# Twenty-eight projection groups ahead of the first attention score, bounded due times in the planner, and gated slots in program order, in a two-layer decoder trunk

## The chip, the cores and the metric

The kernel runs on one core of one Trainium2 chip. The metric is the device time of one execution in microseconds; less is better. Times are given as the median of several runs. One further execution was recorded by the hardware profiler; all rows quoted below come from such a record. The engines are TensorE (PE; its weight loads are PEld), VectorE (DVE), ScalarE (ACT), GpSimd (POOL) and SyncE (SP), whose queue issues the DMAs.

## The reference, cut to what matters

The input is x of 1024 tokens by 1024 features, 256 memory tokens, and weights, all fp32. Two layers follow each other. Layer 0 mixes by native sparse attention with 12 heads of 64 in two groups: queries and six key and value sets are projected, queries and keys are rotated, and each query attends to compressed blocks, to selected blocks and to a window. Layer 1 mixes by forgetting attention over shared keys and values. Both layers attend with four further heads to the memory tokens, project the heads' output, and end with a gated feed-forward part whose up-projection is followed by a causal convolution of width 3.

```python
proj = h @ w_in                                  # 1024 x 1024 by 1024 x A_IN
q = rope(proj[..., :MIX_W].reshape(B, S, 12, 64), pos)
...
s = jnp.einsum('btghd,bngd->bghtn', qc, kc).astype(jnp.float32) * scale
p_cmp = masked_softmax(s, cmp_end[None, :] <= t[:, None])
...
return g[..., 0:1] * o_cmp + g[..., 1:2] * o_slc + g[..., 2:3] * o_win
```

## The kernel before, in words

**Arithmetic.** Every fp32 operand of a matmul is kept as a high and a low part. ScalarE writes the high part (`upper`, L86), VectorE the low part (`lower`, L92). `mm3` (L166, L167, L168) adds three matmuls, high by high, high by low, low by high. One such triple over one of eight tiles of the contraction is called a group here; it is 128 x 512 of output.

**Stages.** Per layer: a projection, the attention, a seam that holds the output projection and prepares the feed-forward part, the gated up-projection (`Up.run`), and the down-projection (`Down`). Layer 0's projection is `layer0_proj` and its attention `attention0`.

**Layer 0's attention.** The projection ahead of it makes keys, values and the first block of queries, rotates them (VectorE L1056, L1057, L1062, POOL L1063), stores them to DRAM (SP L1067) and loads them in another layout (kk by L1258, vv by L1265, qq by L1273). A unit of attention is then a row of tiles: scores (TensorE L316), a lift that masks and takes the maximum (VectorE L356), exponentials (ScalarE L376), weighing by the inverse sums (POOL L411), transposes of the probabilities (TensorE L448) whose result is split into parts (ScalarE L459, VectorE L462), and products with the values (TensorE L475).

The next query blocks (q1, q2) and the memory queries (m0, m1) are projected inside the attention: 96 groups as filler between scores and products. `advance()` puts the next group into the list. Before the first unit, four are put at each early step; afterwards the rest is spread evenly over the steps. Each block of such filler brings its weight loads (L710), conversions, a rotation (VectorE L739, POOL), and stores (SP).

**The planner.** `attention0` and `seam` do not issue instructions at once. They add nodes to an `Order`: engine, assumed cost, due time, the nodes to come after, and the buffers held. `play` then simulates the five engines with these costs and picks for each engine, among the nodes that are ready first, the one due first. The nodes are issued in the order that results, and TensorE, VectorE, ScalarE and GpSimd keep it. SP's queue is placed by the framework from the order of issue.

**The gated up-projection.** It makes the tiles of `Up.run` in slots, seven products per column pair (`product(n, 0)` to `product(n, 6)`), each of four groups. The first four products of columns 0 and 1 are made in the seam. The two halves p and c of a column's accumulator live in psa, of which there are two. `place_early` copies the first sum to its place on GpSimd (L2007), `copied` takes an accumulator half out on ScalarE (L1980). Weight sums come from GpSimd (L1939, L1940, L1946, L1947) and are converted by ScalarE and VectorE. TensorE's order in these slots is chosen by the framework's scheduler, which may interleave products.

Of the kernel before, what the change touches and what calls it, by code (L numbers as in the profile page):

```python
# [44 lines left out]
class Trunk:  # L45
# [590 lines left out]
    def attention0(self, ap, cpool, h, w, od, units, work, spare, lead, lag=2):  # L636
# [142 lines left out]
        def begin(it):  # L779
# [63 lines left out]
            if "norm" in it:  # L843
                i0, i1 = it["norm"]
                brs = u["branches"][i0:i1]
                inv = o.add("DVE", 0.18, lambda: self.invert(u, i0, i1), lambda: min(firsts[id(b), i].due for b in brs for i in b["spans"]) - 3,
# [101 lines left out]
        parts = list(ahead())  # L948
        first = min(it["at"] for it in items)
# [342 lines left out]
    def seam(self, l, oT, pool, fx, up):  # L1292
# [120 lines left out]
        def turn(t):  # L1413
# [17 lines left out]
            c = o.add("POOL", 1.35, lambda: gt(half(u, 0), half(t, 1), half(u, 0), ALU.subtract), due("t3", 6.5 - u), [b])  # L1431
            d = o.add("POOL", 1.35, lambda: gt(half(u, 1), half(u, 1), half(t, 1), ALU.subtract), due("t4", 6.5 - u), [b, s["raw", u, 1]])
# [16 lines left out]
        def sums_21(n, due, behind=()):  # L1449
# [10 lines left out]
            a = o.add("POOL", 1.35, one, due, [lb, *behind], [h, hb], early=20.0)  # L1460
            s["21", n] = o.add("POOL", 1.35, two, due, [a, la], [h, ha], early=20.0)

        def sums_34(n, due):
# [10 lines left out]
            a = o.add("POOL", 1.35, one, due, [la, lb], [h, ha, hb], early=20.0)  # L1474
            s["34", n] = o.add("POOL", 1.35, two, due, [a, s["21", n]], [h, ha, g], early=20.0)
# [421 lines left out]
class Up:  # L1897
# [110 lines left out]

    def third(self, n):
        s = self.st[n]  # L2010
        self.prod(n, s["p"], "s2", "t2", False)
        s["c2"] = self.copied(s["p"])
# [64 lines left out]
    def run(self, late, down):  # L2077
# [28 lines left out]
        for slot in range(7 * NF + 13):  # L2106
            for f in todo.pop(slot, ()):
                f()
            for n in (slot // 7 - 1, slot // 7):
                i, odd = divmod(slot - 7 * n, 2)  # L2110
                if 0 <= n < NF and not odd and done.get(n, 0) <= i < 7:
                    self.product(n, i)
            if slot >= 7 * NF + 6:
                down.step()
# [109 lines left out]
class Hold:  # L2224

    def __init__(self, tag):
        self.tag, self.users, self.left, self.taken = tag, [], 0, False
# [9 lines left out]
class Order:  # L2237

    SHARED = 0.6
    HOP = {"SP": 2.3, "PE": 0.23, "ACT": 0.15, "DVE": 0.14, "POOL": 0.08}  # L2240

    def __init__(self, room):
        self.room, self.nodes, self.queue = room, [], {}

    def hold(self, tag, keep=False):
        h = Hold(tag)
        if tag != "psb":
            self.queue.setdefault(tag, []).append(h)
        h.left = 10 ** 9 if keep else 0
        return h  # L2250

    def held(self, tag):
        h = Hold(tag)
        h.taken = True
# [3 lines left out]
    def add(self, eng, cost, fn, due, after=(), holds=(), early=10.0, slow=False):  # L2258
        n = Node(eng, cost, fn, due, [a for a in after if a is not None], early, slow)
        for h in holds:  # L2260
            h.users.append(n)
            h.left += 1
# [3 lines left out]

    def seen(self, n, eng):

        return n.end + (0.0 if n.eng == eng != "SP" else self.HOP[n.eng])

    def play(self):

        left, free = {}, {}
        for n in self.nodes:
            if callable(n.due):
                n.due = n.due()
            left.setdefault(n.eng, []).append(n)
# [3 lines left out]
        slots = {t: [0.0] * k for t, k in self.room.items()}  # L2281
        drift, out = 0.0, []
        while any(left.values()):
            best = None
            for eng, ns in left.items():
                ready = []
                for n in ns[:160]:
# [5 lines left out]
                    if any(h.tag in self.queue and h not in self.queue[h.tag][:want.count(h.tag)] for h in takes):  # L2293
# [3 lines left out]
                    for x in set(want):  # L2297
                        t = max(t, sorted(slots[x])[want.count(x) - 1])
# [8 lines left out]
            n.start, n.end = t, t + n.cost  # L2307
# [4 lines left out]
            for h in n.holds:  # L2312
                if not h.taken:
                    h.taken = True
                    slots[h.tag].remove(min(slots[h.tag]))
                    if h.tag in self.queue:
                        self.queue[h.tag].remove(h)
                h.left -= 1
                if h.left == 0:
                    slots[h.tag].append(max(self.seen(u, None) for u in h.users))  # L2320
# [61 lines left out]
```

## Time and profile before

| what | us |
|---|---|
| median of 3 runs | 2527.55 |
| lowest and highest of them | 2522.82, 2528.29 |
| profiled execution, its own time | 2525.68 |
| its span in the trace | 2523.7 |
| TensorE busy | 2430.8 |
| VectorE busy | 1875.6 |
| ScalarE busy | 1352.6 |
| GpSimd busy | 730.7 |

A row of a timeline gives start, length, engine, line, operation, output<-inputs and tile, and in brackets how long the engine stood idle before and what ended that. A row of windows gives a stretch of the span, its length, the busy time and count of PE, PEld, DVE, ACT and POOL, then TensorE's granted clock as a share of full speed, the share of time in which the DMA engines were busy, and GB/s. A row on waits gives the engine and line that waited, what it waited for, the total, the number of times and the longest. Matmuls overlap, so the step from start to start is shorter than the length of one.

### The profile page before, as it was taken

How to read it: one execution, taken by the hardware profiler on the slowest of the kernel's cores; microseconds unless marked ns; L12 is line 12 of the kernel's file. 1: busy time of each engine (PE TensorE's matmuls, PEld its weight loads, DVE VectorE, ACT ScalarE, POOL GpSimd, SP SyncE). 2: the span in 40 equal slices, each digit the busy share in tenths (PEclk: the TensorE clock that was granted, in tenths of full speed). 3: DMA queues.
4: the chain of work that ended last, by engine and by line, in shares of the span. 5: the costliest groups of instructions: out<-in, count | busy, mean ns of one | idle time of the engine just before them, and what ended most of it. 6: DMA issues, size and time to landing. Idle time of an engine off the chain costs nothing. (4 is left out here: it accounts for less than half of the span.)

```text
span 2523.7 us, 35482 instructions
## 1 busy us (share of the span) xinstructions
PE 2430.8 (96%) x12210; PEld 2042.2 (81%) x12210; DVE 1875.6 (74%) x3182; ACT 1352.6 (54%) x2583; POOL 730.7 (29%) x620
## 2 busy tenths in 40 slices
PE   7969999998989999999999999998999999999998
PEld 6768888887778888888889988887777888888886
DVE  5747888887487787879765467878577777788765
ACT  5325888886354544544454356756255444445444
POOL 0103455555145554540000000000225455451000
PEclk9989999999999999999999999999999999999999
DMA  8464233245613333358335566765613333238533
GB/s 250 141 193 144 60 84 87 78 133 158 209 59 104 105 112 97 100 177 303 92 126 157 151 187 194 200 177 182 230 76 96 100 100 113 92 109 306 170 95 123
DMA packets 303276, 357.68 MB, mean 142 GB/s; under 512 B 38024, under 2 KB 183288, under 8 KB 303096
## 3 DMA queue, kind: packets, MB, share of 16 engines
q1 hardware_dynamic: 303096, 355.41, 44.8%
q8 instruction: 97, 1.59, 0.3%
q14 instruction: 83, 0.68, 0.1%
HBM read 245.55 MB, written 109.78 MB: 141 GB/s over the span
## 5 line engine op out<-in xcount | busy, mean ns | idle before, releaser
L2046 DVE SCALAR_TENSOR_TENSOR v<-u,cw,v 128x1023 f32<-128x1023 f32 (+1 forms) x176 | 270.6, 1537 | 67.8 <-ACT v L2044 66.1
L86 ACT ACTIVATE wh<-wr 128x512 fp32r<-128x512 f32 (+2 forms) x244 | 182.2, 751 | 240.8 <-PE psa L168 109.7
L92 DVE TENSOR_TENSOR wl<-wr,wh 128x512 fp32r<-128x512 f32 (+2 forms) x244 | 228.5, 940 | 110.3 <-ACT wh L86 110.0
L462 DVE TENSOR_TENSOR pt<-psb,pt 128x512 fp32r<-128x512 f32 (+2 forms) x380 | 246.3, 659 | 61.8 <-ACT pt L459 59.8
L2044 ACT ACTIVATE v<-u,cw 128x1024 f32<-128x1024 f32 x88 | 109.6, 1245 | 308.1 <-DVE u L2033 282.6
L459 ACT ACTIVATE pt<-psb 128x512 fp32r<-128x512 f32 (+2 forms) x380 | 214.2, 576 | 107.4 <-PE psb L448 104.0
L166 PE MATMUL psa<-hT,wh 128*128 128x512 f32 x560 | 218.9, 391 | 12.5 <-ACT wh L86 9.5
L475 PE MATMUL psb<-pt,vv 128*128 128x512 f32 (+2 forms) x864 | 218.5, 354 | 8.3 <-DVE pt L462 6.1
L168 PE MATMUL psa<-hT,wl 128*128 128x512 f32 x560 | 218.0, 389 | 0.8 <-DVE wl L92 0.8
L167 PE MATMUL psa<-hT,wh 128*128 128x512 f32 x560 | 218.2, 390 | 0.0
L316 PE MATMUL psa<-kk,qq 128*128 128x512 f32 (+4 forms) x792 | 176.4, 342 | 24.9 <-DMA qq<-qd 20.2
L356 DVE CUSTOM_DVE_ANT_0 ps<-psa,caub 128x128 f32<-128x128 f32 (+1 forms) x192 | 139.7, 751 | 36.6 <-PE psa L316 26.4
L376 ACT ACTIVATE ps<-ps,stat 128x128 f32<-128x128 f32 (+1 forms) x192 | 148.0, 776 | 27.9 <-DVE stat L356 27.5
L475 PEld LDWEIGHTS psb<-pt,vv 128*128 128x128 f32 x864 | 136.9, 189 | 26.9 <-DVE pt L462 11.8
L316 PEld LDWEIGHTS psa<-kk,qq 128*128 128x128 f32 x792 | 123.4, 192 | 43.2 <-issue 20.2
L166 PE MATMUL psb<-hT,wh 128*128 128x512 f32 x384 | 157.5, 410 | 0.4 <-DVE pt L462 0.4
L130 POOL TENSOR_TENSOR rs<-ss,consts 128x1 f32<-128x1 f32 x24 | 13.3, 555 | 491.5 <-DVE ss L128 319.5
L168 PE MATMUL psb<-hT,wl 128*128 128x512 f32 x384 | 151.8, 395 | 0.0
L167 PE MATMUL psb<-hT,wh 128*128 128x512 f32 x384 | 151.4, 394 | 0.0
L448 PE MATMUL psb<-consts,ps 128*128 128x128 f32 x928 | 146.3, 274 | 3.7 <-POOL ps L411 1.3
L539 POOL TENSOR_TENSOR wr<-wr 128x512 f32<-128x512 f32 x16 | 22.1, 1386 | 408.3 <-ACT wh L216 240.7
L166 PE MATMUL psa<-hx,wh 128*128 128x512 f32 x352 | 138.6, 394 | 0.0
(320 smaller groups left out, 6773.7 us busy)
## 6 DMA issues: line engine op xcount, KB each, us to landing
wr<-in_w_up_dram SPq DMA_DIRECT2D x88, 512.0 KB
wr<-gd SPq DMA_DIRECT2D x154, 256.0 KB
gd<-v SPq DMA_DIRECT2D x88, 256.0 KB
o<-ob SPq DMA_DIRECT2D x128, 128.0 KB
wr<-o SPq DMA_DIRECT2D x32, 512.0 KB
hT<-in_w_down_dram SPq DMA_DIRECT2D x64, 256.0 KB
gd<-gs SPq DMA_DIRECT2D x60, 256.0 KB
qd<-st SPq DMA_DIRECT2D x56, 256.0 KB
```

The lines of the kernel that those rows point to most:

```text
L86: self.nc.scalar.activation(hi, src, AF.Copy)
L92: self.nc.vector.tensor_tensor(lo, src, f32(hi), ALU.subtract)
L166: mm(out, lh, rh, start=first, stop=False, skip_group_check=more)
L167: mm(out, lh, rl, start=False, stop=False, skip_group_check=more)
L168: mm(out, ll, rh, start=False, stop=last, skip_group_check=more)
L316: nc.tensor.matmul(out, w, rhs, start=b not in banks[:i], stop=b not in banks[i + 1:])
L376: nc.scalar.activation(p, p, AF.Exp, bias=st[:, 0, ii:ii + 1], scale=-1.0, accum_out=st[:, 1, ii:ii + 1])
L448: nc.tensor.transpose(tp[0:kb, x:x + P], br["pt"][ii][:, o:o + kb], self.ident)
L459: nc.scalar.activation(st["hi"], st["src"], AF.Copy)
L462: self.nc.vector.tensor_tensor(st["lo"], st["src"], f32(st["hi"]), ALU.subtract)
L475: self.nc.tensor.matmul(out, v, t, start=st["begin"] and i == 0, stop=st["end"] and i == len(mms) - 1)
L2046: nc.vector.scalar_tensor_tensor(v[:, d:], u[:, :S - d], cw[:, tap, i:i + 1], v[:, d:], ALU.mult, ALU.add)
```

## The change

There are three parts.

**The front of layer 0's attention.** Ahead of the first unit a node without instructions is added for SP (assumed cost 12, due at -1), and 28 groups of filler are put into TensorE's list by `advance()`. The weights of a query block are fetched two units of planner time earlier.

```
-                d = o.add("SP", 0.45, fetch, now, holds=[wr], early=14.0)
+                d = o.add("SP", 0.45, fetch, now - 2, holds=[wr], early=14.0)
...
         parts = list(ahead())
+        o.add("SP", 12.0, lambda: None, -1.0)
+        for _ in range(28):
+            advance()
         first = min(it["at"] for it in items)
```

On TensorE, at the end of the projection ahead of the attention, the rows before are these (psb_1593 is the last projection, hT the normalized input, kk and qq keys and queries):

```order
L167 MATMUL psb_1593<-hT_92,wh_1124 128x512
L168 MATMUL psb_1593<-hT_91,wl_1125 128x512
L316 MATMUL psa_1703<-kk_261_1660,qq_265_1674 128x128
L316 MATMUL psa_1703<-kk_261_1660,qq_266_1675 128x128
L316 MATMUL psa_1703<-kk_261_1660,qq_265_1674 128x256
L316 MATMUL psa_1703<-kk_261_1660,qq_266_1675 128x256
L316 MATMUL psa_1703<-kk_261_1660,qq_265_1674 128x384
L316 MATMUL psa_1703<-kk_261_1660,qq_266_1675 128x384
L316 MATMUL psa_1713<-kk_261_1660,qq_265_1674 128x512
L316 MATMUL psa_1713<-kk_261_1660,qq_266_1675 128x512
L166 MATMUL psb_1727<-hT_89,wh_1710 128x512
```

At the same place they are now these (psb_1675, psb_1701, psb_1742 and psb_1795 are the filler's accumulators; of 84 filler matmuls the first three and the last three are shown):

```order
L168 MATMUL psb_1593<-hT_91,wl_1125 128x512
L166 MATMUL psb_1675<-hT_89,wh_1664 128x512
L167 MATMUL psb_1675<-hT_90,wh_1664 128x512
L168 MATMUL psb_1675<-hT_89,wl_1665 128x512
...
L166 MATMUL psb_1795<-hT_91,wh_1669 128x512
L167 MATMUL psb_1795<-hT_92,wh_1669 128x512
L168 MATMUL psb_1795<-hT_91,wl_1670 128x512
L316 MATMUL psa_1823<-kk_278_1768,qq_271_1721 128x128
L316 MATMUL psa_1823<-kk_278_1768,qq_272_1722 128x128
```

The first score stood directly behind the projection; now 84 filler matmuls stand between them. From the first score to the first L448 there are 48 groups before and after; behind that, 48 were left before and 20 are left now.

On SP, at the same place, the rows before (qd<-st stores the rotated queries; the others load):

```order
L1258 DMA kk_261_1660<-kd_80 32x1024 x2
L1067 DMA qd_79<-st_1639 128x512 x2
L1067 DMA qd_79<-st_1647 128x512 x2
L1258 DMA kk_261_1660<-kd_80 32x1024 x2
L1258 DMA kk_262_1665<-kd_80 32x8x128 x4
L1265 DMA vv_1670<-vd_81 128x8x128
L1265 DMA vv_1672<-vd_81 128x8x128
L1273 DMA qq_265_1674<-qd_79 32x512
L1273 DMA qq_266_1675<-qd_79 32x512
```

And now, where kk_278 is kk0, kk_277 is kk1, and seven loads of qq stand between the cos table and kk_277, of which the first two are shown:

```order
L661 DMA wr_1926<-in_a_w_in_dram 128x8x128
L1276 DMA qq_271_1721<-qd_79 32x512
L732 DMA sin_1716<-in_rope_dram 128x512
L1070 DMA qd_79<-st_1639 128x512 x2
L1070 DMA qd_79<-st_1647 128x512 x2
L732 DMA cos_1714<-in_rope_dram 128x512
L1276 DMA qq_272_1722<-qd_79 32x512
L1276 DMA qq_271_1721<-qd_79 32x512
...
L1261 DMA kk_277_1753<-kd_80 32x8x128 x4
L1261 DMA kk_278_1768<-kd_80 32x1024 x4
```

Behind the stores stood six loads of kk, two of vv and eight of qq; now a cos table, seven loads of qq and eight of kk stand there, and the loads of vv come later.

On VectorE the low parts of the first two weight blocks (wl, L92, four instructions) stood behind the first lift L356 and now stand among the last conversions of the projection. The first lift now stands behind the rotation (L739) of the first three filler accumulators, two instructions of each.

**The planner.** The assumed cost of the inversion goes from 0.18 to 0.30, those of GpSimd's sums in the seam from 1.35 to 1.6, and the share by which a busy GpSimd lengthens a VectorE node from 0.6 to 1.0. Due times are bounded by successors before the simulation, and among the nodes of an engine (SP excepted) that are ready within 0.1 of the first, the one due first is taken. `rounds` is 0, so that `lateness` is not used.

```
-    SHARED = 0.6
+    SHARED = 1.0
...
+    def backward(self):
+
+        late = {}
+        for n in reversed(self.nodes):
+            if n.eng == "PE":
+                begin = n.due - n.cost
+            else:
+                if n in late:
+                    n.due = min(n.due, late[n] - n.cost * (1 + self.margin))
+                begin = n.due
+            for a in n.after:
+                late[a] = min(late.get(a, 1e9), begin - self.hop(a, n.eng))
...
-                    t0 = min(t for t, _ in ready)
+                    t0 = min(t for t, _ in ready) + (0.0 if eng == "SP" else 0.1)
```

**The gated slots.** `place_early(0)` moves from the start of `Up.run` to slot 8, the copy of column 1's accumulator half (`copy_fourth`) and `place_early(1)` to slot 10, and in the slots 0 to 16 TensorE keeps the order in which the program is written.

```
-        self.place_early(0)
-        self.st[1]["c5"] = self.copied(self.st[1]["c"])
-        self.place_early(1)
...
+        at(8, self.place_early, 0)
+        at(10, self.copy_fourth, 1)
+        at(10, self.place_early, 1)
...
+        with self.k.tc.manual_schedule(engines={mybir.EngineType.PE}):
+            do(range(17))
+        do(range(17, 7 * NF + 13))
```

On TensorE, where the up-projection begins, the rows before (psa_1337 is column 0's accumulator, psa_1342 column 1's; wh_1369 is the high part of a weight sum of column 1):

```order
L168 MATMUL psa_1337_7929<-hT_1348_8012,wl_1352_8035 128x512
L166 MATMUL psa_1342_7957<-hT_1348_8012,wh_1369_8162 128x512
L167 MATMUL psa_1342_7957<-hT_1348_8012,wh_1369_8162 128x512
L166 MATMUL psa_1337_7929<-hx_1322_7839,wh_1351_8034 128x512
L167 MATMUL psa_1337_7929<-hx_1322_7839,wh_1351_8034 128x512
L168 MATMUL psa_1337_7929<-hx_1322_7839,wl_1352_8035 128x512
```

And now, with psa_1382 the accumulator of column 2; of the 12 matmuls of each of the last three products the first or the last is shown:

```order
L168 MATMUL psa_1337_7929<-hT_1346_7995,wl_1352_8036 128x512
L166 MATMUL psa_1337_7929<-hx_1322_7839,wh_1351_8035 128x512
...
L166 MATMUL psa_1337_7929<-hT_1354_8072,vh_1355_8078 128x512
...
L168 MATMUL psa_1337_7929<-hT_1354_8072,vl_1356_8079 128x512
L166 MATMUL psa_1382_8222<-hx_1296_7630,wh_1373_8187 128x512
```

Column 1's product stood between the products of column 0; now column 0's last two products and column 2's first stand ahead of it.

More of the change, by code (lines that the diff above doesn't have):

```diff
@@ L845, in begin @@
                 brs = u["branches"][i0:i1]
[L846 removed]
+                inv = o.add("DVE", 0.30, lambda: self.invert(u, i0, i1), lambda: min(firsts[id(b), i].due for b in brs for i in b["spans"]) - 3,
                             [x for b in brs for x in b["exps"]], [u["st"]])
@@ L1459, in two @@
                 nc.gpsimd.tensor_tensor(t[:, 0], t[:, 1], st[n]["ra"][:, 0:4], ALU.subtract)
-            a = o.add("POOL", 1.35, one, due, [lb, *behind], [h, hb], early=20.0)
-            s["21", n] = o.add("POOL", 1.35, two, due, [a, la], [h, ha], early=20.0)
+            a = o.add("POOL", 1.6, one, due, [lb, *behind], [h, hb], early=20.0)
+            s["21", n] = o.add("POOL", 1.6, two, due, [a, la], [h, ha], early=20.0)
         def sums_34(n, due):
@@ L1473, in two @@
                 nc.gpsimd.tensor_tensor(st[n]["s34"][:, 1], st[n]["ra"][:, 4:8], st[n]["s21"][:, 0], ALU.subtract)
-            a = o.add("POOL", 1.35, one, due, [la, lb], [h, ha, hb], early=20.0)
-            s["34", n] = o.add("POOL", 1.35, two, due, [a, s["21", n]], [h, ha, g], early=20.0)
+            a = o.add("POOL", 1.6, one, due, [la, lb], [h, ha, hb], early=20.0)
+            s["34", n] = o.add("POOL", 1.6, two, due, [a, s["21", n]], [h, ha, g], early=20.0)
         def halves(n, key, src, names, due, after, holds, keep):
@@ L2105, in run, with do @@
                 at(7 * n + 19, self.store, n // 2)
[L2106 to L2114, printed above, removed]
+        def do(slots):
+            for slot in slots:
+                for f in todo.pop(slot, ()):
+                    f()
+                for n in (slot // 7 - 1, slot // 7):
+                    i, odd = divmod(slot - 7 * n, 2)
+                    if 0 <= n < NF and not odd and done.get(n, 0) <= i < 7:
+                        self.product(n, i)
+                if slot >= 7 * NF + 6:
+                    down.step()
+        with self.k.tc.manual_schedule(engines={mybir.EngineType.PE}):
+            do(range(17))
+        do(range(17, 7 * NF + 13))
         assert not todo
@@ L2224, with __init__ @@
 class Hold:
-    def __init__(self, tag):
-        self.tag, self.users, self.left, self.taken = tag, [], 0, False
+    def __init__(self, tag, keep=False):
+        self.tag, self.keep, self.given, self.users = tag, keep, False, []
 class Node:
@@ L2253, in held @@
         h = Hold(tag)
-        h.taken = True
+        h.given = True
+        self.holds.append(h)
         self.room[tag] -= 1
@@ L2276, in play, with lateness, forward @@
                 n.due = n.due()
+        if self.margin is not None:
+            self.backward()
+        out = best = self.forward()
+        last = lambda order: max(n.end for n in order)
+        length = last(best)
+        for _ in range(self.rounds):
+            self.lateness(out)
+            out = self.forward()
+            if last(out) < length:
+                best, length = out, last(out)
+        return best
+    def lateness(self, out):
+        late, free = {}, {}
+        end = max(n.end for n in out)
+        for n in sorted(out, key=lambda n: (n.end, n.start), reverse=True):
+            at = min(late.get(n, end), free.get(n.eng, end))
+            n.late = at - (n.end - n.start)
+            free[n.eng] = n.late
+            for a in n.after + n.freed:
+                late[a] = min(late.get(a, end), n.late - self.hop(a, n.eng))
+        for n in out:
+            n.due = n.late + (n.cost if n.eng == "PE" else 0.0)
+    def forward(self):
+        left, free = {}, {}
+        queue = {t: list(q) for t, q in self.queue.items()}
+        for h in self.holds:
+            h.taken, h.left = h.given, len(h.users) + (10 ** 9 if h.keep else 0)
+        slots = {t: [(0.0, [])] * k for t, k in self.room.items()}
+        for n in self.nodes:
+            n.end = None
             left.setdefault(n.eng, []).append(n)
@@ L2292, in play @@
                     want = [h.tag for h in takes]
-                    if any(h.tag in self.queue and h not in self.queue[h.tag][:want.count(h.tag)] for h in takes):
+                    if any(h.tag in queue and h not in queue[h.tag][:want.count(h.tag)] for h in takes):
                         continue
@@ L2306, in play @@
             t, n = best
-            n.start, n.end = t, t + n.cost
+            n.start, n.end, n.freed = t, t + n.cost, []
             if n.slow and free.get("POOL", 0.0) > t:
```

33 lines of the change are left out of this document (18 added, 15 removed).

## The prediction

> **What bounds the kernel now.** I read the page's first two parts, then TensorE's waits, then the timeline around the longest wait, then the stretches of the stage behind it.
>
> ```profile
> span 2523.7 us, 35482 instructions
> PE 2430.8 (96%) x12210; PEld 2042.2 (81%) x12210; DVE 1875.6 (74%) x3182; ACT 1352.6 (54%) x2583; POOL 730.7 (29%) x620
> PE   7969999998989999999999999998999999999998
> ```
>
> TensorE is busy for 96% of the span, so the time is its work plus about 93 us of idle, and what runs at a lower clock. Slice 3 (63 us each, so 126 to 189 us) stands out with a 6. The list of TensorE's waits names its largest piece (total, times, longest, in us):
>
> ```profile
> PE psa L316 <- DMA qq<-qd: 20.2, 3, 19.2
> PE psa L166 <- ACT wh L86: 10.1, 3, 4.7
> ```
>
> 19.2 us of waiting are one event, the first score of layer 0's attention. The second row holds a 4.7 us wait in each layer's gated FFN, which the change also touches. The timeline of TensorE shows the first event (start, length, idle before in brackets); of the 22 projection matmuls before it the first and the last stand here:
>
> ```profile
> 163.69 0.39 PE L168 MATMUL psb<-hT,wl 128*128 128x512 f32 x1
> ...
> 168.46 0.39 PE L168 MATMUL psb<-hT,wl 128*128 128x512 f32 x1
> 188.05 2.81 PE L316 MATMUL psa<-kk,qq 128*128 128x128 f32 x8 [19.20 <-DMA qq<-qd]
> 190.66 0.63 PE L166 MATMUL psb<-hT,wh 128*128 128x512 f32 x1
> ...
> 193.22 0.46 PE L166 MATMUL psb<-hT,wh 128*128 128x512 f32 x1
> ```
>
> Matmuls overlap, so a matmul's price is the step from start to start: (168.46 - 163.69) / 21 = 0.227 us before the wait. After it six projection matmuls take 193.22 - 190.66 = 2.56 us, 0.427 each. The windows say why (length, then busy time and count for PE, PEld, DVE, ACT, POOL, then TensorE's granted clock, DMA share, GB/s):
>
> ```profile
> 168.85:188.05 19.20, 0.00 (x1) 0.04 (x1) 2.74 (x4) 1.26 (x2) 2.90 (x2) 0.60 0.67 193
> 188.05:193.30 5.25, 5.25 (x15) 4.43 (x16) 3.26 (x10) 0.00 (x0) 0.00 (x0) 0.50 0.59 196
> 250.00:300.00 50.00, 49.66 (x329) 43.91 (x328) 44.99 (x129) 41.38 (x101) 24.73 (x37) 1.00 0.23 60
> 300.00:350.00 50.00, 49.25 (x329) 43.25 (x328) 45.33 (x135) 43.91 (x109) 23.02 (x32) 1.00 0.22 59
> 240.00:560.00 320.00, 313.09 (x2049) 274.91 (x2049) 280.78 (x811) 267.93 (x675) 159.33 (x215) 0.99 0.32 90
> 560.00:645.00 85.00, 77.45 (x428) 63.28 (x428) 57.90 (x122) 53.76 (x131) 42.10 (x38) 1.00 0.57 178
> ```
>
> In the wait no engine works much; after it TensorE runs at 0.50 for 5.25 us. From 240 to 560 us the attention keeps TensorE 98% busy, so work taken out of there is worth nearly its length, unless another engine takes over.
>
> **The front of the attention.** The change puts 28 groups of the next query projection, 84 matmuls, between the last projection and the first score. At the step above they need 84 x 0.227 = 19.1 us, against 19.2 us of wait. They come out of the steady stage, where the same projection is strewn as filler (count, then first and last start):
>
> ```profile
> L168 PE MATMUL psb<-hT,wl x95: 389/392/628, 192.8 to 547.9; 128*128 128x512 f32 x95
> ```
>
> That is one matmul of each of the 96 groups (one lies just ahead of the window). By the new order 48 groups still stand between the first score and the first transposed block of probabilities (L448), and 20 instead of 48 are strewn through the rest, to the same place near its end.
>
> Can the groups run at once? Their high parts are converted by ScalarE in this trace already before the wait (the four L86 halves at 157.84 to 161.5 us, below). Their low parts move on VectorE from behind the first lift to ahead of the last evictions: three took 1.89 us, so four cost 2.5 us, and VectorE idles 3.48 + 1.61 us there.
>
> ```profile
> 157.84 1.15 ACT L86 ACTIVATE wh<-wr 128x512 fp32r<-128x512 f32 x2 [1.75 <-PE psa L168]
> 160.36 1.16 ACT L86 ACTIVATE wh<-wr 128x512 fp32r<-128x512 f32 x2 [1.37 <-PE psb L167]
> 160.58 0.69 DVE L1056 TENSOR_TENSOR rt<-psb,cos 128x512 f32<-128x512 f32 x1 [3.48 <-PE psb L168]
> 163.48 0.42 DVE L92 TENSOR_TENSOR st<-psa,st 128x256 fp32r<-128x256 f32 x1 [1.61 <-ACT st L86]
> 190.26 1.89 DVE L92 TENSOR_TENSOR wl<-wr,wh 128x512 fp32r<-128x512 f32 x3
> ```
>
> When is the first score ready now? The wait is a chain through SP's queue: stores of the rotated queries, then loads.
>
> ```profile
> 167.99 0.80 SPq L1258 DMA_DIRECT2D kk<-kd  x2
> 171.67 3.55 SPq L1067 DMA_DIRECT2D qd<-st x4
> 175.26 3.55 SPq L1258 DMA_DIRECT2D kk<-kd x6
> 178.85 1.23 SPq L1265 DMA_DIRECT2D vv<-vd x2
> 180.12 6.49 SPq L1273 DMA_DIRECT2D qq<-qd x8
> 186.65 0.42 SPq L732 DMA_DIRECT2D cos<-in_rope_dram x1
> ```
>
> Behind the stores stand 16 issues before and 16 after, of another mix: one cos (0.42), seven qq at 6.49 / 8 = 0.81, eight kk at 3.55 / 6 = 0.59. That is 0.42 + 5.68 + 4.73 = 10.8 us behind 175.2, so 186.1; before, the last issue ended at 186.61 and the score began 1.44 us later. So the loads are there at about 187.5 us, and the groups end at 168.69 + 19.1 = 187.8. The wait is covered to within a fraction of a microsecond. I take 0.5 us left; the bounds are 0 and 2.4, four kk1 loads (4 x 0.59) that now stand ahead of kk0, which the score needs. A further weight load, one qq and a sin table stand ahead of the stores, in place of two kk loads; SP has nothing to issue there between 168.8 and 171.67 us, so they cost nothing. The first lift on VectorE now stands behind two multiplications of a rotation whose tables are loaded behind kk0; tables and the first scores come within about 1.5 us of each other, and TensorE has filler there: nothing, at most 1.5 us.
>
> The clock: without the wait the 5.25 us at 0.50 become 2.6 us. -2.6, or 0 if TensorE goes cold all the same. A rest of 0.5 us is far from both 19.2 and 4.7 us, after which the clock was found at half, so I take -2.6.
>
> **What the steady stage gives back.** 19.1 us of TensorE's work leave it. How much turns into idle is read from two neighbouring windows with unequal filler (projection matmuls alone):
>
> ```profile
> 250.00:300.00 50.00, 7.63 (x27) 4.78 (x27) 0.00 (x0) 0.00 (x0) 1.00 0.23 60
> 300.00:350.00 50.00, 3.44 (x12) 2.11 (x12) 0.00 (x0) 0.00 (x0) 1.00 0.22 59
> ```
>
> With 15 matmuls fewer (3.4 us at 0.227) TensorE's idle goes from 0.34 to 0.75 us, VectorE's busy time only from 44.99 to 45.33, ScalarE's from 41.38 to 43.91. Idle grows by 0.41 / 3.4 = 12% of what is taken out, so 19.1 us cost 2.3. The density after, 20 groups in 320 us, is that of the second window. Bounds: 0, and all 19.1 if VectorE (91% there) or ScalarE (88%) sets the pace. I take 2.3, the row itself.
>
> **The gated FFN.** Before, TensorE stood still in each layer until ScalarE had converted a weight sum; then the clock was 0.50 (TensorE, ScalarE, GpSimd):
>
> ```profile
> 736.52 0.39 PE L168 MATMUL psa<-hT,wl 128*128 128x512 f32 x1
> 741.65 0.79 PE L166 MATMUL psa<-hT,wh 128*128 128x512 f32 x1 [4.74 <-ACT wh L86]
> ...
> 744.53 1.28 POOL L1940 TENSOR_TENSOR ws<-ws,wr 128x512 f32<-128x512 f32 x1
> ...
> 740.55 1.05 ACT L86 ACTIVATE wh<-ws 128x1024 fp32r<-128x1024 f32 x1
> 748.09 1.25 ACT L2044 ACTIVATE v<-u,cw 128x1024 f32<-128x1024 f32 x1 [6.49 <-issue]
> ...
> 750.18 1.05 ACT L86 ACTIVATE wh<-ws 128x1024 fp32r<-128x1024 f32 x1
> 751.13 0.59 ACT L2036 ACTIVATE u<-psa 128x512 f32<-128x512 f32 x1
> 736.80:741.70 4.90, 0.16 (x2) 0.05 (x1) 2.98 (x6) 2.06 (x3) 1.16 (x2) 0.77 0.70 201
> 741.70:746.40 4.70, 4.70 (x11) 3.71 (x12) 1.41 (x2) 0.00 (x0) 3.17 (x3) 0.51 0.42 125
> ```
>
> In program order two products, 24 matmuls, run in that wait: 24 x 0.227 = 5.4 us, until 742.2, or 742.9 if the second waits for its low part. Next stands the first product of another column, which needs the accumulator that ScalarE's u copy frees. On ScalarE that copy stands behind v, wh of the raw weights, and wh of the sums; that last one waits for GpSimd's sum (744.53 + 1.28 = 745.8) and takes 1.05, the copy 0.59: about 747.5. So TensorE waits 742.9 to 747.5, 4.6 us, where it waited 4.74, and starts cold again. The product that was late before comes behind that. I put it at 0 for both layers, with bounds of +4 (each wait 2 us longer) and -14 (each wait and its half-clock stretch, 4.74 + 4.70 / 2 = 7.1, gone twice). Were the clock full behind the moved wait, 2.35 us a layer would be gained and the sum below would be 4.7 lower; the last row, 0.51 behind 4.74 us of rest, is the nearest and says no. [...]
>
> **Order's new rules.** Costs of 1.6 for 1.35, SHARED and the bounded due times only reorder lists. In the seams I find no wait of over 1 us that they free: 0, give or take 2. In the attention's tail TensorE idles 85.00 - 77.45 = 7.5 us; a better or worse order there is worth 0, give or take 4.
>
> **Sum**, against the profiled execution of 2525.68 us (span 2523.7): 19.1 less work behind the first score, +0.5 wait, -2.6 clock, +2.3 given back: -18.9, so 2506.8. The runs' median is 2527.55, 1.9 above; taken from that, 2508.7. I say 2508. About 0.2%, 5 us, is what a measurement of this kernel can tell from no change.
>
> **Rivals.** (A) The filler was free: VectorE at 91% sets the steady stage, and its list is no shorter. Then 13 to 19.1 us come back as idle in place of 2.3: -18.9 + 10.7 = -8.2 to -18.9 + 16.8 = -2.1, 2519 to 2525. For it: VectorE and ScalarE are both near 90%. Against: the second of the two windows.
> (B) More than one wait goes: the gated waits end as well (-14) on top of the front: about 2495. Against: the copy behind the GpSimd sums.
> (C) Slower: in the gated slots in program order TensorE can't pass a late product. If the three products behind the fourth column half (another column's first, the late one, the next) each wait as the first does, 4.6 us with 2.35 us of half clock behind it, twice, that is 3 x 6.95 x 2 = 42 us against 14 before: +28 - 18.9 = +9, about 2537. It turns slower only if the slots' waits together exceed 33 us where they are 14. Against: the accumulator copies are 0.59 us.
> (D) The wait only moves behind the groups: if the loads of kk0 are held up until after the groups by 10 us, those and the clock are lost: -18.9 + 10 + 2.6 = -6.3, about 2521. Against: 16 issues before and after.
>
> **How the numbers follow.** Forecast (gain of 12 to 25 us) 0.63; A 0.14; B 0.12; C 0.05; D 0.06. The range takes in B's near side and most of A: 2496 to 2521, leaving out about 0.06 below and 0.12 above. Faster than by 5 us: the forecast, B, D and a third of A, 0.63 + 0.12 + 0.06 + 0.05 = 0.86; A's rest is the same, 0.09; C slower, 0.05.
>
> **What would show it.** Right: no TensorE wait over 1 us before the first L316 score, clock 1.0 there, idle from 240 to 560 us up by 2 to 3 us over a stage some 17 us shorter. Wrong: a releaser DVE or ACT with tens of short waits in that stage (A); a wait on kk or qq behind the groups (D); the gated wait absent (B) or several of them (C).

## The result, and the profile after

The changed kernel takes 2502.64 us (median of 4 runs, 2501.73 to 2505.03) against 2527.62 us before: a ratio of 0.9906 with a 95% interval of 0.9893 to 0.9918, so 20.7 to 27.0 us less. The two profiled executions differ by 20.65 us (2525.68 and 2505.03). The forecast was 2508 in a range of 2496 to 2521. The total came near; two of its terms did not, and their errors cancelled, as the experiments show.

The first two parts of the page after:

```profile
span 2503.0 us, 35524 instructions
PE 2428.3 (97%) x12210; PEld 2040.0 (82%) x12210; DVE 1884.3 (75%) x3182; ACT 1351.8 (54%) x2583; POOL 737.0 (29%) x620
PE   7999999998989999999999999998999999999998
```

The 6 in the slice around the first score is now a 9. TensorE's longest waits after (total, times, longest, in us; the first row was there before, with 13.5 us):

```profile
PE psb L159 <- DVE xn L144: 13.6, 2, 10.5
PE psa L166 <- DVE u L2036: 5.4, 2, 2.7
...
PE psa L316 <- DMA qq<-qd: 1.3, 2, 0.9
```

The 19.2 us row is gone, and so are the 4.7 us waits on wh in the gated part; waits of 2.7 us on another line stand in their place. The timeline of TensorE after, at the first score:

```profile
188.14 0.39 PE L168 MATMUL psb<-hT,wl 128*128 128x512 f32 x1
188.37 1.03 PE L316 MATMUL psa<-kk,qq 128*128 128x128 f32 x6
189.24 0.39 PE L166 MATMUL psb<-hT,wh 128*128 128x512 f32 x1
```

There is no bracket: the score follows the last of the 84 matmuls at the ordinary step of 0.23 us. The timeline of SP's queue after, around the same place:

```profile
172.34 3.59 SPq L1070 DMA_DIRECT2D qd<-st  x4
175.97 0.44 SPq L732 DMA_DIRECT2D cos<-in_rope_dram  x1
176.47 3.42 SPq L1276 DMA_DIRECT2D qq<-qd  x7
179.94 4.62 SPq L1261 DMA_DIRECT2D kk<-kd  x8
184.67 0.36 SPq L732 DMA_DIRECT2D cos<-in_rope_dram  x1
```

The last load for the score is issued by 184.56 us, 1.5 us earlier than the 186.1 that the prediction worked out, because seven qq loads took 0.49 each and not 0.81. The windows of the kernel after show that the wait was filled at full clock, and what the attention took from the first score to the first transpose of the seam (L1526 at 636.53 us):

```profile
169.20:188.30 19.10, 19.10 (x86) 15.67 (x84) 8.11 (x11) 4.32 (x8) 5.92 (x4) 1.00 0.75 216
188.37:636.53 448.16, 433.99 (x2693) 375.31 (x2693) 371.91 (x1022) 344.52 (x857) 214.31 (x270) 0.99 0.42 122
```

The same stretch before (its first score to L1523 at 656.42 us):

```profile
188.05:656.42 468.37, 453.58 (x2777) 391.18 (x2777) 379.73 (x1032) 347.80 (x863) 219.57 (x272) 0.99 0.40 119
```

2777 - 2693 = 84 matmuls are gone from it, 19.1 us, and it is 20.2 us shorter. From its end to the end of the kernel the two profiles differ by only 0.8 us (1867.3 and 1866.5), so the gain lies in the attention. Read alone, that says that the steady stage gave nearly nothing back. It does not say why.

### The profile page after: what moved, and what is told of

It is laid out like the page before. It is cut to its first block, busy times and chain, and to the rows that moved or that the text cites. A ratio compares the mean times of both kernels' runs of the same rounds, so it can differ in the third digit from the quotient of the medians.

```text
span 2503.0 us, 35524 instructions
## 1 busy us (share of the span) xinstructions
PE 2428.3 (97%) x12210; PEld 2040.0 (82%) x12210; DVE 1884.3 (75%) x3182; ACT 1351.8 (54%) x2583; POOL 737.0 (29%) x620
## 4 chain that ended last, share of the span: by engine, by line
PE 80%; DVE 8%; DMA 4%; ACT 3%; issue 2%; POOL 1%; SPq 1%; POOLq 0%; DVEq 0%; ACTq 0%
PE psa L166 12%; PE psa L167 12%; PE psa L168 12%; PE psb L166 10%; PE psb L168 9%; PE psb L167 9%; PE psa L316 5%; PE psb L448 5%; PE psb L475 5%; DVE hT L92 1%; DVE wl L92 1%; DVE pt L462 1%; ACT ps L376 1%; DMA wr<-o 1%; ACT pt L459 1%
## 5 line engine op out<-in xcount | busy, mean ns | idle before, releaser
L2052 DVE SCALAR_TENSOR_TENSOR v<-u,cw,v 128x1023 f32<-128x1023 f32 (+1 forms) x176 | 276.7, 1572 | 67.7 <-ACT v L2050 66.1
L92 DVE TENSOR_TENSOR wl<-wr,wh 128x512 fp32r<-128x512 f32 (+2 forms) x244 | 229.2, 944 | 112.6 <-ACT wh L86 112.3
L376 ACT ACTIVATE ps<-ps,stat 128x640 f32<-128x640 f32 (+4 forms) x192 | 147.7, 773 | 28.7 <-DVE stat L356 28.5
L448 PE MATMUL psb<-consts,ps 128*128 128x128 f32 x928 | 145.9, 274 | 6.6 <-DVE pt L462 1.7
L356 DVE CUSTOM_DVE_ANT_0 ps<-psa,caub 128x128 f32<-128x128 f32 (+1 forms) x192 | 139.6, 750 | 15.2 <-PE psa L316 13.4
```

What stands on the lines that cost most here:

```text
L92: self.nc.vector.tensor_tensor(lo, src, f32(hi), ALU.subtract)
L376: nc.scalar.activation(p, p, AF.Exp, bias=st[:, 0, ii:ii + 1], scale=-1.0, accum_out=st[:, 1, ii:ii + 1])
L448: nc.tensor.transpose(tp[0:kb, x:x + P], br["pt"][ii][:, o:o + kb], self.ident)
L2052: nc.vector.scalar_tensor_tensor(v[:, d:], u[:, :S - d], cw[:, tap, i:i + 1], v[:, d:], ALU.mult, ALU.add)
```

## The experiments

front_only, no_groups, old_gated and old_planner take the change apart; the kernels behind them take the planner and the gated slots apart. All times are medians, each with its ratio to the kernel before, which was measured again beside them on the same chip: 2525.32 us beside the first four, 2526.68 beside no_bounds, no_tolerance, old_costs and groups_20 (another chip), 2525.87 beside the last four. So rows are compared by their ratios. "Attention" is the stretch from the first score to the seam's first transpose in the profiled execution. The column behind it says how much of that stretch ran at a granted clock of 0.5, by the trace's record of the clock.

| kernel | us | ratio, 95% interval | attention, us | of it at half clock, us | groups ahead of the first score |
|---|---|---|---|---|---|
| before | 2527.62 | 1 | 468.37 | 8.7 | 0 |
| changed | 2502.64 | 0.9906 (0.9893 to 0.9918) | 448.16 | 10.2 | 28 |
| front_only | 2516.05 | 0.9962 (0.9948 to 0.9977) | 452.50 | 0.0 | 28 |
| no_groups | 2514.81 | 0.9955 (0.9941 to 0.9970) | 461.88 | 13.2 | 0 |
| old_gated | 2503.85 | 0.9910 (0.9894 to 0.9927) | 448.21 | 6.8 | 28 |
| old_planner | 2516.18 | 0.9963 (0.9948 to 0.9978) | 454.38 | 6.8 | 28 |
| no_bounds | 2523.86 | 0.9987 (0.9978 to 0.9996) | 461.75 | 13.7 | 28 |
| no_tolerance | 2512.45 | 0.9939 (0.9924 to 0.9954) | 448.19 | 3.4 | 28 |
| old_costs | 2509.08 | 0.9932 (0.9917 to 0.9947) | 450.57 | 10.2 | 28 |
| groups_20 | 2512.40 | 0.9941 (0.9925 to 0.9958) | 454.87 | 13.7 | 27 |
| after_again | 2504.33 | 0.9914 (0.9900 to 0.9929) | 445.54 | 3.4 | 28 |
| early_release | 2503.80 | 0.9913 (0.9898 to 0.9928) | 444.85 | 3.4 | 28 |
| bounds_gpsimd | 2525.68 | 0.9997 (0.9987 to 1.0007) | 462.67 | 17.1 | 28 |
| bounds_vector | 2514.06 | 0.9951 (0.9936 to 0.9966) | 450.48 | 10.2 | 28 |

The changed kernel's attention program was profiled four times (changed, old_gated, after_again, early_release): 444.9 to 448.2 us, so differences of up to 3.4 us in that column are not told apart. Much of this spread is the clock. A projection matmul took 0.427 us at a clock of 0.50 behind the first score of the kernel before, against 0.227 ahead of the wait, so I take about half of such time as lost; with half of the last but one column taken off, the four are 443.0 to 444.8 us. Below, "with the clock set apart" means this estimate.

**front_only.** The kernel before with the front part alone.

```
+        o.add("SP", 12.0, lambda: None, -1.0)
+        for _ in range(28):
+            advance()
```

> The kernel before with the front part alone: the SP node, the 28 groups ahead of the first score and the weight loads two units earlier; planner rules, costs and gated slots as before. If the groups in the wait are the whole gain, the 19.2 us wait and the half clock behind it are gone and the time is 20 to 22 us below before, about 2506. If the new planner rules are what keeps TensorE busy once the filler is thin, the steady stage gives back some 10 us here and the time is about 2517, with waits on VectorE and ScalarE between 240 and 540 us.

Measured: 2516.05 us, 9 below before. That is the time of the second theory, but not its mechanism, as the numbers below and the next run show. The windows of front_only, the first 6 us and the whole attention:

```profile
189.82:195.82 6.00, 5.78 (x31) 4.84 (x32) 3.83 (x11) 0.00 (x0) 0.00 (x0) 1.00 0.90 311
...
189.82:642.32 452.50, 434.58 (x2692) 370.92 (x2693) 373.32 (x1023) 343.12 (x856) 216.21 (x270) 1.00 0.40 120
```

The clock is full, but the stretch is 452.5 us where 468.37 less 19.1 of moved work less 2.6 of half clock would be 446.7. So 5.8 us are given back, not 10, and in old_planner, which runs the same attention program, 7.7 (with the clock set apart 7.6 and 6.1). The score also waited 2.27 us here, until 189.82 in place of 188.05 us. SP's queue shows why:

```profile
181.78 6.66 SPq L1276 DMA_DIRECT2D qq<-qd  x8
```

The loads of qq are the last, issued by 188.44 us, as they were before; in the changed kernel the last load is issued by 184.56. So the new order on SP, which the text on the change shows with the front, is not the front's: it comes from the planner's rules, above all the bounds (in no_bounds, below, the loads of qq are last too, issued by 189.28 us). Another 3.2 us of the loss against the first theory lie behind the attention, and no run explains them; over all 14 profiles that rest of the kernel takes 1864.3 to 1871.7 us.

**no_groups.** The changed kernel without the front part.

> The changed kernel without the front part: no SP node, no groups ahead of the first score, weight loads as before; planner rules, costs and gated slots as changed. If the groups are the gain: the 19 us wait is back with half clock behind it, and the time is 1 to 3 us below before, about 2526. If the planner rules carry the gain: 8 to 12 us below before, about 2517.

Measured: 2514.81 us, 10.5 below before, as the second theory had it. The windows of no_groups:

```profile
185.00:646.88 461.88, 451.94 (x2776) 391.67 (x2776) 376.26 (x1032) 347.31 (x862) 219.36 (x272) 0.99 0.41 123
```

With the same matmuls as before (2776 and 2777 records) the stretch is 6.5 us shorter, and TensorE's idle in it falls from 468.37 - 453.58 = 14.8 to 9.9 us. The first score also came at 185.00 us in place of 188.05. So the planner's rules are worth 6.5 us in the attention (8.7 with the clock set apart) and 3 ahead of it, without any group moved. They act in the steady stage. From 60 us behind the first score to 130 us ahead of the seam, before and in no_groups:

```profile
248.05:526.42 278.37, 272.60 (x1798) 240.43 (x1795) 244.86 (x699) 231.72 (x577) 136.80 (x189) 0.99 0.30 81
```

```profile
245.00:516.88 271.88, 271.58 (x1817) 241.52 (x1815) 246.11 (x712) 235.78 (x595) 136.10 (x189) 1.00 0.31 84
```

The whole 6.5 us are here, and TensorE's idle falls from 5.8 to 0.3 us. TensorE's waits between the first score and 560 us, of no_groups:

```profile
PE psb L475 <- DVE pt L462: 1.2, 3, 0.7
...
PE psb L448 <- POOL pw L411: 0.3, 1, 0.3
```

and of the kernel before in the same stretch:

```profile
PE psb L448 <- POOL pw L411: 1.8, 4, 0.8
PE psa L316 <- DVE stat L356: 1.6, 4, 0.9
PE psb L475 <- DVE pt L462: 1.5, 3, 0.8
```

The waits on the weighing (L411) shrink from four to one, and those on the lift (L356) are not in the list of no_groups at all.

**old_gated.** The changed kernel with the early copies at the start of the slots (not shown) and with TensorE's order there left to the framework's scheduler.

```
-        with self.k.tc.manual_schedule(engines={mybir.EngineType.PE}):
-            do(range(17))
-        do(range(17, 7 * NF + 13))
```

> The changed kernel with the gated slots as before (early copies at the start, order of the slots left to the scheduler). If the moved wait costs what it did, 0 to 1 us above the changed kernel, about 2503. If the gated part gains by keeping the clock full (its waits of 2.7, 0.8, 0.7 and 0.3 us leave the clock at 1.00 where one of 4.7 us left it at 0.51), 2.35 us a layer more: about 5 us above the changed kernel, 2507 to 2508, with a 4.7 us wait at clock 0.5 in each layer.

Measured: 0.9910, within the interval of the changed kernel (0.9906 and, again, 0.9914). The 5 us of the second theory did not come, and the whole time cannot tell the gated part from nothing. The windows of 12 us behind the wait, of old_gated and then of the kernel after:

```profile
720.33:732.33 12.00, 12.00 (x45) 9.43 (x46) 6.94 (x8) 6.08 (x7) 5.11 (x4) 0.86 0.25 74
```

```profile
720.15:732.15 12.00, 10.16 (x41) 7.43 (x42) 8.72 (x6) 9.26 (x11) 8.64 (x5) 1.00 0.30 83
```

At a clock of 0.86 and without waits in the one, at 1.00 with waits in the other. Do these traces price the part? The 361st matmul behind the last transpose (L1611; L1608 in the kernel before) starts 92.5 us after it in both layers of old_gated, 91.2 in both of the changed kernel, and 91.3 and 91.6 in after_again: about 1 us a layer. But with the old planner the sign is not the same: 91.4 and 90.8 in the kernel before and 92.5 and 93.4 in front_only, both with the slots unchanged, 92.5 and 94.1 in old_planner with the slots changed. So 1 us a layer is not shown to be the slots' own.

**old_planner.** The changed kernel with the old planner and its old costs.

> The changed kernel with the planner's class and costs as before (no bounded due times, no 0.1 tolerance, SHARED 0.6, GpSimd sums 1.35, inversion 0.18); front and gated slots as changed. If the planner rules only reorder lists: within 2 us of the changed kernel, 2501 to 2505. If they hide the thinner filler: about 10 us above, 2512, with idle in the steady stage.

Measured: 2516.18 us, 9 below before and 12 to 13 above the changed kernel, as the second theory had it. The groups alone give 9 us, the planner alone 10.5 with the gated part, both together 21 to 25: they add up as nearly as the runs can tell.

**no_bounds, no_tolerance, old_costs** take one of the planner's three edits out of the changed kernel each.

The bounds:

```
-    def __init__(self, room, rounds=0, margin=1.0):
+    def __init__(self, room, rounds=0, margin=None):
```

The tolerance:

```
-                    t0 = min(t for t, _ in ready) + (0.0 if eng == "SP" else 0.1)
+                    t0 = min(t for t, _ in ready) + 0.0
```

The costs (one of six sums; the inversion goes back to 0.18 as well):

```
-            a = o.add("POOL", 1.6, one, due, [lb, *behind], [h, hb], early=20.0)
+            a = o.add("POOL", 1.35, one, due, [lb, *behind], [h, hb], early=20.0)
...
-    SHARED = 1.0
+    SHARED = 0.6
```

> The changed kernel without the bounded due times (margin None); tolerance, costs, front and gated slots as changed. The run with the old planner was 12 to 13 us above the changed kernel. If the bounds carry that: 8 to 12 us above the changed kernel, 2511 to 2515, with idle of 6 us or more in the attention between 250 and 510 us. If they do not: within 2 us of it, 2503 to 2505.

> The changed kernel without the 0.1 tolerance in the choice of the next node. If the bounds carry the planner's gain: within 2 us of the changed kernel, 2503 to 2505. If the tolerance is needed for the due times to decide at all (without it the node that is ready first by a hair goes first whatever its due time): 5 to 10 us above, 2508 to 2513.

> The changed kernel with the assumed costs as before (SHARED 0.6, GpSimd sums 1.35, inversion 0.18); bounds, tolerance, front and gated slots as changed. If the costs are fine print: within 2 us of the changed kernel, 2503 to 2505. If the lengthening of VectorE beside GpSimd is what makes the order fit the chip: 5 us or more above, with waits on VectorE in the attention.

Measured: without the bounds nearly the whole gain is gone, 2523.86 us and 461.75 us of attention, more than either theory allowed. Without the tolerance the attention is as in the changed kernel (448.19), and with the old costs it is 450.57 (with the clock set apart 446.5 and 445.4, where the changed kernel has 443.0 to 444.8), so by the attention the first theory of each nearly holds. By the whole time the second does: by their ratios the two are some 4 to 8 us slower than the changed kernel's two measurements, with intervals that overlap them in part, while their profiled spans (2505.9 and 2506.6) lie only 3 to 4 above its 2503.0. What the other runs lost, the profiles do not show. So the bounds carry the gain beside the other two edits, and what those are worth stays open; no run has the bounds alone. no_bounds is also worse than old_planner (461.75 against 454.38, with the clock set apart 454.9 against 451.0), which has no bounds either. So the tolerance and the new costs do harm without bounds, and part of what the bounds win is that harm undone; how was not tried.

The timelines of VectorE and TensorE in no_bounds show one such place:

```profile
306.30 1.28 DVE L92 TENSOR_TENSOR wl<-wr,wh 128x1024 fp32r<-128x1024 f32 x1 [2.13 <-ACT wh L86]
307.51 0.81 DVE L356 CUSTOM_DVE_ANT_0 ps<-psa,caub 128x640 f32<-128x640 f32 x1
...
308.38 1.08 PE L316 MATMUL psa<-kk,qq 128*128 128x512 f32 x4 [1.36 <-DVE stat L356]
```

VectorE stands still 2.13 us in front of a weight conversion of the filler, whose high part ScalarE has not made yet; the lift stands behind it in VectorE's list, and TensorE waits 1.36 us for the lift to free its accumulator.

**bounds_gpsimd, bounds_vector.** Bounds for the nodes of one engine only.

```
-                if n in late:
+                if n in late and n.eng == "POOL":
```

and, in the other run,

```
-                if n in late:
+                if n in late and n.eng == "DVE":
```

> The changed kernel with due times bounded for GpSimd's nodes alone. Without any bounds the attention from the first score to the seam takes 461.8 us, with all of them 448.2. If the weighing on GpSimd, whose due times are set per step and not by its transposes, is what the bounds put right: most of the 13.6 us is there, 449 to 453 us, and the time within 5 us of the changed kernel. If it is VectorE's order between filler rotations and the chain from lift to inversion: 458 to 462 us, and 10 us or more above the changed kernel.

> The changed kernel with due times bounded for VectorE's nodes alone. If the bounds on GpSimd carry the gain: the attention takes 458 to 462 us, 10 us or more above the changed kernel. If VectorE's do: 449 to 453 us, within 5 us of it.

I had expected GpSimd; it is VectorE. The windows of bounds_gpsimd and of bounds_vector over the attention:

```profile
190.93:653.60 462.67, 440.79 (x2693) 378.83 (x2694) 377.15 (x1023) 345.76 (x856) 217.26 (x270) 0.98 0.40 117
```

```profile
190.71:641.19 450.48, 435.94 (x2693) 375.92 (x2693) 373.03 (x1023) 344.53 (x856) 216.38 (x270) 0.99 0.41 121
```

Bounds on GpSimd leave 21.9 us of idle, as without any (22.5); bounds on VectorE bring it to 14.5, as with all (14.2). Of the other 4.9 us between the two rows, TensorE's longer busy time for the same 2693 matmuls, 3.4 are half clock by the table, (17.1 - 10.2) / 2. The busy time of VectorE hardly differs (377.15 and 373.03): the order of its list is what changed. Bounds on ScalarE or SP alone were not tried. In whole time bounds_vector is still some 10 us above the changed kernel, outside the 5 that I had allowed, and its ratio, 0.9951, is not told apart from old_planner's 0.9963: its first score waits 2.98 us, and its seams hold waits of 2.2 and 2.4 us in each layer, with a clock of 0.75 and 0.74 over the 12 us behind them.

**groups_20.** `range(28)` becomes `range(20)`.

> The changed kernel with 20 groups in place of 28 ahead of the first score. The loads for the score are there at about 186.2 us and the 20 groups end at about 183, so a wait of some 3.2 us opens. Waits of 3.0 to 3.1 us left the clock at 0.82 to 0.87 over the 12 us that follow, one of 2.7 us left it at 1.00. If it falls here too: 3.2 us of wait and 2.6 of half clock, less 1.6 to 2.3 that the eight groups left in the steady stage save of idle: 3 to 5 us above the changed kernel, 2506 to 2508. If the clock holds: about 1 us above, 2504.

Measured: 2512.40 us, above both theories. The kernel was not what I meant: the planner put 27 groups ahead of the first score by itself. The score came at 186.63 us with a wait of 0.19. The wait opened one block later. VectorE and TensorE in groups_20:

```profile
190.63 0.69 DVE L739 TENSOR_TENSOR rt<-psb,cos 128x512 f32<-128x512 f32 x1 [2.60 <-DMA cos<-in_rope_dram]
...
193.37 1.73 PE L316 MATMUL psa<-kk,qq 128*128 128x192 f32 x10 [3.12 <-DVE stat L356]
194.89 0.68 PE L166 MATMUL psb<-hT,wh 128*128 128x512 f32 x1
```

The lift stands on VectorE behind a rotation of the filler that waits for its cosine table; TensorE waits 3.12 us for the lift and is cold afterwards (0.43 us from the projection matmul at 195.37 us to the next, 0.23 ahead of the wait). This is the risk that the prediction had priced at "nothing, at most 1.5 us". In the changed kernel the rotation waits 1.75 us for that table, and TensorE still has filler then. The run does not answer how the gain grows with the number of groups.

**early_release, with after_again as its control.** ScalarE copies the fourth half out, VectorE adds later, and one conversion moves a slot back.

```
-            add(s["ub"][:, CH:], s["p"], s["c5"], ALU.add)
+            if n < 1:
+                self.k.nc.scalar.activation(s["ub"][:, CH:], s["p"], AF.Copy)
+                add(s["ub"][:, CH:], s["ub"][:, CH:], s["c5"], ALU.add)
...
-                    at(7 * n + slot, f, n)
+                    at(7 * n + slot + (n == 2 and f == self.split_21), f, n)
```

> The changed kernel once more, as a control on the same chip as the three below: 20 to 25 us below before, 2502 to 2507.

> The changed kernel with the first gated column released earlier: its fourth half is copied out by ScalarE, which idles 7 us there, and VectorE adds the other sum afterwards in SBUF; and the conversion of the next column's weight sums is put one slot later, so that ScalarE's copy that frees the accumulator does not stand behind GpSimd's sum. If the 2.7 us wait is VectorE's list of conversions and the next 0.7 the copy behind the sum: both go, 1.5 to 2.3 us a layer, 3 to 5 us below the changed kernel, with the first wait under 0.8 us. If the weight loads set the pace of these slots (GpSimd's sums wait for them): the waits only move behind, within 1 us of the changed kernel.

Measured: 0.9913 and, for after_again, 0.9914, no difference. TensorE's waits in early_release:

```profile
714.90 0.50 PE L166 MATMUL psa<-hx,wh 128*128 128x512 f32 x1 [2.19 <-ACT u L2037]
718.80 0.51 PE L166 MATMUL psa<-hT,vh 128*128 128x512 f32 x1 [0.88 <-DVE u L2043]
722.53 0.50 PE L166 MATMUL psa<-hx,wh 128*128 128x512 f32 x1 [0.69 <-ACT u L2046]
```

The first wait is 2.19 us here (1.1 in the second layer), now on ScalarE's copy, and the one behind the sums still is 0.69. In the changed kernel the first wait was 2.71 in both layers, but in after_again, the same program, 1.40, so the edit is not shown to have shortened it. The first theory fails; the second is right on the time and names the wrong cause for the first wait. The timeline of ScalarE in early_release shows that the copy itself came late:

```profile
714.25 0.60 ACT L2037 ACTIVATE u<-psa 128x512 f32<-128x512 f32 x1 [6.28 <-DVE hT L92]
```

The product that it copies was done by 712.7 us (last start 712.33), and ScalarE had been idle for 6.28. The trace names VectorE's conversion hT (L92) of the seam as the releaser: u is written only once x has been read. That u lies in the place of x would explain it; that was not tried. The two profiles of the unedited kernel point the same way: VectorE's read of the accumulator (L2036) begins 21.84 us behind the last transpose in the first and 21.85 in after_again, where TensorE came 1.3 us later and waited 1.3 us less. So the wait lies in the chain that ends the seam, and no version beat the changed kernel.

## Why the prediction was right, and where it was not

**The wait at the first score: right.** The 84 matmuls filled it at 0.227 us each, the score was ready in time, and the clock stayed at 1.00, so -2.6 us as forecast. The experiments add a condition: the loads are in time only in the order that the bounded planner gives them. Under the old planner the score waited 2.3 to 2.4 us behind the groups, and with no bounds or with those of one engine 2.6 to 3.0.

**What the steady stage gives back: mis-sized.** The term was 2.3 us, 12% of what is moved, from two neighbouring windows. front_only and old_planner gave back 5.8 and 7.7 us; under the new planner no_groups (461.88, with a clock of 0.50 in the 6 us behind the first score, so 3.0 lost) less 19.1 is 439.8 us, against 444.9 to 448.2: 5.1 to 8.4. So 27 to 44%; with the clock set apart it is 6.1 to 8.6 us in all of these. Two windows of 50 us hold different phases of the attention, and I read a slope from two points. Two more windows of the same trace show none:

```profile
400.00:450.00 50.00, 49.71 (x333) 44.68 (x332) 44.70 (x137) 41.77 (x104) 23.72 (x35) 1.00 0.26 73
450.00:500.00 50.00, 48.54 (x316) 42.27 (x315) 45.11 (x131) 43.37 (x110) 26.36 (x38) 1.00 0.25 69
```

They hold 21 and 22 matmuls of filler, and idle of 0.29 and 1.46 us. Of what is given back, 3.1 us (front_only against before) and 4.2 us (changed against no_groups) are idle of TensorE in the attention. The rest stands in no list of waits. That filler between dependent steps hides waits too short to be seen as idle would explain it; this was not tried.

**The planner's rules: mis-sized.** "Order's new rules ... only reorder lists" was the step that failed. I priced them at 0, with 2 for the seams and 4 for the tail, and looked for single waits of over 1 us that they could free. They gave 6.5 us in the attention without groups and 4 to 10 with them. What they freed were many waits of 0.3 to 0.9 us in the steady stage, where I had allowed them nothing, and the loads ahead of the first score.

**The sum: right by two errors.** Give-back was 3 to 6 us too low, and the planner's term too high by the 4 to 10 us that it gave. The attention's predicted change, -19.1 - 2.6 + 2.3 = -19.4, met -20.2. Without the experiments the profile after would have confirmed a wrong account: the idle in the attention, 14.8 us before and 14.2 after, is the sum of both. One sign that I had named for being right did not come: the idle of the steady stage was to rise by 2 to 3 us. It fell from 5.8 us to 258.16 - 254.54 = 3.6:

```profile
248.37:506.53 258.16, 254.54 (x1711) 224.06 (x1710) 237.99 (x696) 228.43 (x578) 128.04 (x179) 1.00 0.31 83
```

In front_only, without the new rules, it was 6.8. Rival (A) had 13 to 19.1 us come back; 5 to 9 did, with the new rules and without them.

**The gated slots: total right, course wrong.** The prediction let two products run in the wait and then put one wait of 4.6 us, cold. TensorE, VectorE and ScalarE after:

```profile
717.05 0.39 PE L168 MATMUL psa<-hT,wl 128*128 128x512 f32 x1
720.15 0.50 PE L166 MATMUL psa<-hx,wh 128*128 128x512 f32 x1 [2.71 <-DVE u L2036]
723.97 0.51 PE L166 MATMUL psa<-hT,vh 128*128 128x512 f32 x1 [0.79 <-DVE u L2039]
727.74 0.50 PE L166 MATMUL psa<-hx,wh 128*128 128x512 f32 x1 [0.73 <-ACT u L2042]
...
713.58 4.11 DVE L92 TENSOR_TENSOR hT<-x,hT 128x512 fp32r<-128x512 f32 x3
...
719.41 0.68 DVE L2036 TENSOR_TENSOR u<-psa,c 128x512 f32<-128x512 f32 x1
...
727.12 0.57 ACT L2042 ACTIVATE u<-psa 128x512 f32<-128x512 f32 x1
```

I had missed that both halves of a column lie in one accumulator: the second product may not write its half until VectorE has read the other, and that read stands in VectorE's list behind the seam's last conversions, three of which took 4.11 us (early_release suggests that x must be read first in any case). So the wait comes first, 2.71 us, and then 0.79, 0.73 and 0.32 us, 4.55 in all, close to the 4.6. The last copy ends at 727.7, and 747.5 less the 18 to 20 us that the kernel is ahead by then (last transposes and seam's start) is 727.5 to 729.5: that chain was worked out to within 2 us. Divided into four, the wait left the clock at 1.00 here, over the 12 us from 720.15 us, where the prediction had TensorE start cold. That was luck: in groups_20's second layer the same wait was 2.72 us, and the 12 us behind it ran at 0.88.

## What to carry to other kernels

Filler that is moved into a long wait is not free where it came from: price it by a run that moves it alone, not by two windows of one trace; here 5 to 9 of 19.1 us came back. Where a planner orders the work, a rule that only reorders lists can be worth as much as the work that is moved: here 9 us from the groups alone and 10.5 from the planner with the gated slots. With due times bounded by what the successors need, the order on VectorE, which both the filler and the critical chain use, mattered most in the attention, and bounds for VectorE alone did not give the whole time. A total that comes out as forecast proves no term; take the change apart, one part at a time and each part alone.

## What the hardware showed that I had not expected

The clock fell after rests shorter than I had allowed for, and not at a fixed length. In front_only TensorE waited 2.27 us for the first score and the next 6 us ran at 1.00 (row above); in old_planner the same wait was 2.43 us:

```profile
189.34:195.34 6.00, 6.00 (x22) 4.95 (x23) 4.08 (x11) 0.00 (x0) 0.00 (x0) 0.72 0.87 307
```

In the gated slots 2.87 us of rest in old_costs left the 12 us behind it at 1.00, while 2.86 us in bounds_gpsimd's second layer left them at 0.75, and 3.06 us in old_gated at 0.86. Two rests of 2.21 and 2.42 us with 0.5 us of work between them, in bounds_vector's seam, were followed by a clock of 0.75; the window takes the 12 us behind the second:

```profile
708.56:720.56 12.00, 12.00 (x41) 9.68 (x42) 12.00 (x11) 5.39 (x10) 8.34 (x5) 0.75 0.00 0
```

In bounds_gpsimd the same rest was 2.88 us in the first layer and 2.86 in the second of one execution, and the clock held behind the one and fell behind the other; the windows take the 12 us behind each:

```profile
736.60:748.60 12.00, 10.26 (x41) 7.51 (x42) 8.72 (x6) 9.29 (x11) 8.66 (x5) 1.00 0.31 85
1903.50:1915.50 12.00, 10.01 (x29) 6.92 (x30) 6.27 (x5) 7.04 (x9) 6.63 (x5) 0.75 0.30 83
```

So the length of the rest alone does not divide the cases, and these runs do not show what does. A rest that leaves the clock at 1.00 in one place can cost time in another: a mean of 0.88 (groups_20) or 0.75 (here) over 12 us is up to 1.4 or 3.0 us by my estimate, 12 x 0.12 and 12 x 0.25.
